# Up products of a two-stream feed-forward network by seven products in place of eight, on one Trainium2 core

## The chip, the cores and the metric

The kernel runs on one core of one Trainium2 chip. The metric is the device time of one execution in microseconds, as a median of several runs. In what follows TensorE is PE in the profile, VectorE is DVE, ScalarE is ACT, GpSimd is POOL, and SP issues the transfers. Weight loads of TensorE have a row of their own, PEld.

## The reference, cut to what matters

Two networks run one after the other on 512 tokens of width 1024, in fp32. The second works on two streams, X (512 tokens) and a context C (256 tokens). The part that is changed is the feed-forward network of its first layer, which both streams pass through with the same weights:

```python
def conv_ffn(h, w_up, conv, w_down):
    u = dwconv(h @ w_up, conv)          # 3 taps along the tokens, for each channel
    a, g = jnp.split(u, 2, axis=-1)     # 2 x 2816 channels
    return (jax.nn.silu(g) * a) @ w_down

x = x + g1 * y                          # y, yc: the convolution mixers
x = x + g2 * conv_ffn(modulate(rmsnorm(x, norm_ffn[l]), sh2, sc2), w_up[l], w_conv_ffn[l], w_down[l])
if not last:
    xc = xc + cg1 * yc
    xc = xc + cg2 * conv_ffn(modulate(rmsnorm(xc, norm_ffn[l]), csh2, csc2), w_up[l], w_conv_ffn[l], w_down[l])
```

Ahead of it are the mixers (their last product is `out`), behind it a windowed attention (`gqa`) in which C gives keys and values, and then the last feed-forward network, on X alone.

## The kernel before, in words

Every fp32 value that enters a matmul is held as two parts, high and low, and each product of two values is made by three matmuls (high by high, high by low, low by high: `mm3`). A split into parts is a cast (mostly on ScalarE) and a subtraction on VectorE (`split`). Activations lie with the channels on the 128 partitions, in 8 tiles of 128 channels, and the tokens in the columns.

The 2816 hidden channels are 22 units of 128. In `ffn` (line 1352) unit j needs two weight tiles of 1024 columns (`wload`: a transfer, a cast, a subtraction), and for gate and up 8 x 3 matmuls each, with 512 columns for X and 256 for C. The first two units (`HALVED`) run X in two halves of 256 columns. `act` makes the convolution out of PSUM (one scaled copy on ScalarE, two multiply-adds on VectorE), the silu, the product and the split. The units are taken in groups of 8, 7 and 7 (`GROUPS`); `down(g)` multiplies a group by its down weights, and each of its 8 x 2 results is added onto the residual (`resid`, VectorE). In the last group the last three output columns run C first, then X's first half, then its second half, so that the norm ahead of the attention (`modnorm`: statistics by `stat`, a reciprocal root `rstd`, its broadcast by TensorE `rstd_bc`, and the tiles `h_mod`) can start early.

The last feed-forward network, on X alone, already makes 17 of its 22 units by Strassen's method: X's tokens are two halves, the 1024 channels two halves, gate and up are the two halves of the weights, and seven products of sums take the place of eight (`wload7`, `products7`, lines 734 and 879). The 7 products are 7 x 4 x 3 matmuls. Sums of weights are made by VectorE for every unit, sums of activations once (`mod7`).

The order on the engines isn't the order of the code: all operations are recorded (class `Rec`) and listed by their dependences, with a modelled cost and a priority of their own for each. Weight splits have a bias of -1000000, `ahead(CHAIN)` puts chains to the norm first. All instructions bear the line of the one place that issues them (L385). `arenaR` holds split values, `arenaZ` and `arenaF` others, in addresses worked out for each stage (`phase`, `hold`, `t`); all transfers go through SP's queue.

Of the kernel before, what the change touches and what calls it, by code (L numbers as in the profile page):

```python
# [8 lines left out]
F32 = mybir.dt.float32  # L9
# [23 lines left out]
ROUNDS = 7  # L33
PLAIN = 5
WO1_AT = (2, 3, 5, 7)
SM_SCALE = 0.125
# [40 lines left out]
def _layout(i):  # L77
# [72 lines left out]
    o["wup1"] = fm(f("w_up_2")[1])  # L150
    o["wdn0"] = down(f("w_down_2")[0])
    o["wdn1"] = down(f("w_down_2")[1])
# [359 lines left out]
class Ker:  # L512
# [69 lines left out]
    def t(self, pool, shape, tag, dt=F32, bufs=1):  # L582

        n = 1
        for x in shape:
            n *= x
        c = self.hold(pool, n, tag, dt, bufs)
        m, off, n0, bufs, i = c
        assert n <= n0, (tag, n, n0)
        c[4] += 1  # L590
        o = off + (i % bufs) * (-(-n0 // GR) * GR)
# [141 lines left out]

    def wload7(self, src1, src2):
# [4 lines left out]
        a, b, c = (self.slot() for _ in range(3))  # L739
        d = [self.t("ph", [512], "whi22", F32R), self.t("z", [512], "wlo22", F32R)]  # L740
        s12, s34 = (self.t("ph", [1024], "wsum", bufs=2) for _ in range(2))
# [136 lines left out]

    def products7(self, st, w, one, two):


        nc = self.nc
        V = nc.vector
        x, y, z = (self.ps()[:, :TC] for _ in range(3))

        def product(p, n, first):
            (hi, lo), b = w[n - 1], st.b7[n - 1]
            for k in range(4):
# [3 lines left out]
        def keep(p):  # L892
            t = self.t("ph", [TC], "keep", bufs=4)
            nc.scalar.copy(t, p)
            return t

        def add(out, p, t):
            V.tensor_tensor(out=out, in0=p, in1=t, op=ALU.add)

# [6 lines left out]
        product(y, 3, False)  # L906
        add(one[:, TWO], y, s2)
        product(x, 7, False)
        add(two[:, TWO], x, s5)
        product(z, 2, True)  # L910
        add(one[:, ONE], z, s1)
        product(x, 4, False)
        nc.scalar.copy(two[:, ONE], x)

# [444 lines left out]
    def ffn(self, streams, wu, wd, conv=None, gate=None, post=None, mid=None, seven=None):  # L1359
# [5 lines left out]
        if True:  # L1365
# [3 lines left out]
            def up(j):  # L1369
                if seven is not None and j >= PLAIN:  # L1370
                    w = self.wload7(wu[j + NH - first], wu[j + first])
                    pu, pg = (self.t("ph", [S], "ft512", bufs=7) for _ in range(2))
                    self.products7(X, w, pu, pg)
                    acts[X, j] = self.act(None, X, pg, pu, j, conv, "z")
# [107 lines left out]
    def gqa(self, X, C, cfg):  # L1482
# [260 lines left out]
    def mixers(self, X, C):  # L1743
# [3 lines left out]
        if True:  # L1747
# [65 lines left out]
            def out(half):  # L1813
                order = [(mp, st) for mp in range(1 if half else 4) for st in streams]
# [3 lines left out]
                for mp, st in order:  # L1818
                    if mp not in ws:
# [4 lines left out]
                    for m2 in range(2):  # L1824
                        m = 2 * mp + m2
                        p = self.ps()[:, :st.T]
                        for k in range(4):
                            sl = slice(k * 256 + m2 * P, k * 256 + (m2 + 1) * P)
                            self.mm3(p, (hi[:, sl], lo[:, sl]), y[st, 4 * half + k], k == 0, k == 3)
                        self.resid(st, m, p, gate(st, m))  # L1830
                        if half:
                            self.stat(st, m)
                            if st is C and m == 2:
                                self.modnorm(X, 0, 1, ALL, ("mq512", 2))

# [38 lines left out]
    def run(self):  # L1874
# [59 lines left out]
        C.x = [xc[:, k, :] for k in range(KT)]  # L1934
        C.h = [(hc[0][:, k, :], hc[1][:, k, :]) for k in range(KT)]
        if start >= 5:
            load_x(lambda k: self.stat(X, k))
# [6 lines left out]
        if start <= 6:  # L1944
            self.phase({"g": list(range(8))}, (2 * KT * TC, KT * TC), 4)
            self.modnorm(C, 0, 1)
            self.segment("R")
            self.ffn([X, C], a["wup0"], a["wdn0"], conv="cf0",
                     gate=lambda st, m: self.modp[0][:, st.cond, 5, m:m + 1],
                     post=lambda st, m, tk: self.stat(st, m, tk), mid=lambda st, tk: self.modnorm(st, 1, 0, tk))  # L1950
        if stop == 6:
# [92 lines left out]
```

## Time and profile before

| what | value |
|---|---|
| median of three runs | 2578.2 us (2577.62 to 2578.24) |
| the profiled execution | 2579.19 us, of which 2577.4 us is the span |
| mean granted clock of TensorE | 0.997 |
| TensorE, matmuls | 2543.6 us, 99% |
| TensorE, weight loads | 2288.3 us, 89% |
| VectorE | 1964.1 us, 76% |
| ScalarE | 1304.7 us, 51% |

The two-stream feed-forward network lies between about 1370 and 1950 us of the span, the last one between about 2170 and 2570 us. In a group of matmuls the mean duration of one counts its pipelined end; the distance from one start to the next is shorter. A time behind an arrow is idle time of the engine ahead of an instruction, and what ended it.

### The profile page before, as it was taken

Reading aid. Unit: us, or ns where it says so; the run is one execution under the profiler, and the core shown is the slowest. Engines: PE = TensorE matmul, PEld = TensorE weight load, DVE = VectorE, ACT = ScalarE, POOL = GpSimd, SP = SyncE. Lnnn points to the kernel's source line nnn. Section 1 sums busy time; section 2 is a strip of 40 time slices with the busy share of each in tenths; the row PEclk is TensorE's granted clock in tenths of the full one; section 3 lists DMA queues with packets and bytes.
Section 4 is the critical chain, followed back from the end, with each engine's and each line's share of the span. In section 5 each row is a group of like instructions: output and inputs, shape, how many; then the busy total and the mean of one; then the engine's idle time right before and its main releaser. Section 6 shows DMA issues by size and latency. Waiting matters only on the chain.

```text
span 2577.4 us, 40702 instructions
## 1 busy us (share of the span) xinstructions
PE 2543.6 (99%) x15878; PEld 2288.3 (89%) x15878; DVE 1964.1 (76%) x3691; ACT 1304.7 (51%) x2481; POOL 130.7 (5%) x252
## 2 busy tenths in 40 slices
PE   8999999999999999999999999999999999999998
PEld 8998988889979888889888988888889988998997
DVE  8888999845898999448986754453457799997977
ACT  6877522224896322236664432231335798554644
POOL 0000000000010000004740000000000000000000
PEclk9999999999999999999999999999999999999999
DMA  4112566522124666321121121211112101223322
GB/s 148 56 62 72 190 211 221 181 94 78 58 66 153 206 222 197 117 93 60 58 74 55 57 66 66 66 62 65 63 56 66 50 26 50 92 78 95 123 89 84
DMA packets 73345, 252.92 MB, mean 98 GB/s; under 512 B 8512, under 2 KB 10688, under 8 KB 72768
## 3 DMA queue, kind: packets, MB, share of 16 engines
q1 hardware_dynamic: 73152, 250.32, 29.9%
q8 instruction: 124, 2.03, 0.3%
q14 instruction: 69, 0.57, 0.1%
HBM read 248.19 MB, written 2.10 MB: 97 GB/s over the span
## 4 chain that ended last, share of the span: by engine, by line
PE 92%; DVE 3%; POOL 2%; ACT 2%; issue 1%; DMA 0%; POOLq 0%; SPq 0%; DVEq 0%; ACTq 0%
PE psum_t L385 92%; POOL arenaZ L385 2%; DVE arenaF L385 2%; DVE arenaR L385 1%; ACT arenaF L385 1%; ACT arenaR L385 1%; DMA arenaF<-in_wup_dram 0%; ACT L383 0%; DMA arenaF<-in_xT_dram 0%; ACT L385 0%; DMA out_dram<-arenaF 0%; ACT arenaZ L385 0%; DVE psum_t L385 0%; DVE arenaZ L385 0%; POOLq L385 0%
## 5 line engine op out<-in xcount | busy, mean ns | idle before, releaser
L385 PE MATMUL psum_t<-arenaR 128*128 128x256 f32 (+2 forms) x13755 | 2352.0, 327 | 13.4 <-ACT arenaR L385 8.0
L385 PEld LDWEIGHTS psum_t<-arenaR 128*128 128x128 f32 x13755 | 2041.1, 189 | 240.0 <-ACT arenaR L385 9.7
L385 ACT CAST arenaR<-arenaF 128x1024 fp32r<-128x1024 f32 (+4 forms) x552 | 482.1, 881 | 740.2 <-PE psum_t L385 566.3
L385 DVE TENSOR_TENSOR arenaR<-arenaF,arenaR 128x1024 fp32r<-128x1024 f32 (+4 forms) x519 | 540.3, 1049 | 92.9 <-ACT arenaR L385 88.9
L385 ACT ACTIVATE arenaF<-arenaF 128x256 f32<-128x256 f32 (+10 forms) x809 | 428.7, 547 | 202.3 <-DVE arenaF L385 169.8
L385 DVE SCALAR_TENSOR_TENSOR arenaF<-psum_t,arenaF 128x511 f32<-128x511 f32 (+4 forms) x348 | 211.2, 611 | 247.1 <-PE psum_t L385 125.3
L385 DVE TENSOR_TENSOR arenaF<-arenaF 128x512 f32<-128x512 f32 (+5 forms) x503 | 266.5, 544 | 28.7 <-ACT arenaF L385 21.2
L385 DVE TENSOR_TENSOR arenaF<-psum_t,arenaF 128x512 f32<-128x512 f32 (+1 forms) x287 | 163.1, 576 | 137.8 <-PE psum_t L385 136.1
L385 PE MATMUL psum_t<-arenaZ,arenaR 128*128 128x256 f32 (+3 forms) x1261 | 261.7, 313 | 2.4 <-DVE arenaF L385 1.5
L385 DVE CUSTOM_DVE_ANT_0 arenaF<-arenaF 128x1024 f32<-128x1024 f32 x192 | 245.9, 1281 | 8.9 <-DMA arenaF<-in_wmod_dram 3.5
L385 PEld LDWEIGHTS psum_t<-arenaZ,arenaR 128*128 128x128 f32 x1261 | 189.2, 188 | 18.7 <-DVE arenaF L385 2.8
L385 ACT CAST arenaR<-psum_t 128x512 fp32r<-128x512 f32 (+3 forms) x333 | 157.6, 479 | 30.8 <-PE psum_t L385 27.6
L385 ACT ACTIVATE arenaF<-psum_t,arenaF 128x256 f32<-128x256 f32 (+3 forms) x170 | 85.9, 519 | 114.5 <-PE psum_t L385 105.4
L385 DVE SCALAR_TENSOR_TENSOR arenaF<-arenaF 128x256 f32<-128x256 f32 (+8 forms) x346 | 137.8, 421 | 4.7 <-ACT arenaF L385 3.0
L385 POOL TENSOR_TENSOR arenaZ<-arenaZ,arenaF 128x256 f32<-128x256 f32 x120 | 104.1, 869 | 446.9 <-DVE arenaF L385 423.6
L385 PE MATMUL psum_t<-arenaF 128*128 128x128 f32 (+2 forms) x730 | 113.7, 268 | 6.7 <-DVE arenaF L385 5.2
L385 DVE CUSTOM_DVE_ANT_0 arenaF<-psum_t,arenaF 128x256 f32<-128x256 f32 (+3 forms) x208 | 103.6, 511 | 11.7 <-PE psum_t L385 9.9
L385 DVE TENSOR_TENSOR arenaR<-psum_t,arenaR 128x512 fp32r<-128x512 f32 (+4 forms) x169 | 98.7, 590 | 12.1 <-ACT arenaR L385 10.6
L385 POOL COPY arenaF<-arenaF 128x1 f32<-128x1 f32 x128 | 26.4, 231 | 1595.1 <-DVE arenaF L385 1171.1
L385 PEld LDWEIGHTS psum_t<-arenaF 128*128 128x128 f32 x730 | 90.0, 152 | 17.4 <-DVE arenaF L385 6.2
L385 ACT ACTIVATE arenaR<-arenaF 128x256 fp32r<-128x256 f32 (+1 forms) x168 | 81.5, 523 | 31.9 <-DVE arenaF L385 24.9
L385 DVE SCALAR_TENSOR_TENSOR arenaR<-arenaF,arenaR 128x256 fp32r<-128x256 f32 (+1 forms) x164 | 77.7, 505 | 7.4 <-ACT arenaR L385 7.2
(49 smaller groups left out, 534.4 us busy)
## 6 DMA issues: line engine op xcount, KB each, us to landing
arenaF<-in_wmod_dram SPq DMA_DIRECT2D x96, 512.0 KB, 4.2
arenaF<-in_wgu_dram SPq DMA_DIRECT2D x88, 512.0 KB, 3.5
arenaF<-in_wup_dram SPq DMA_DIRECT2D x88, 512.0 KB, 3.4
arenaF<-in_wqkv_dram SPq DMA_DIRECT2D x35, 512.0 KB, 3.5
arenaF<-in_wd_dram SPq DMA_DIRECT2D x32, 448.0 KB, 3.2
arenaF<-in_wdn_dram SPq DMA_DIRECT2D x32, 448.0 KB, 3.2
arenaF<-in_wab_dram SPq DMA_DIRECT2D x20, 512.0 KB, 3.5
arenaF<-in_wd_dram SPq DMA_DIRECT2D x16, 512.0 KB, 4.2
```

The costliest lines, as they stand in the source:

```text
L385: getattr(getattr(self.nc, e), fn)(*a, **k)
```

## The change

X and C are joined to 768 columns, two halves of 384 (256 of X and 128 of C each). Three units are made plainly on the halves, nineteen by the seven products (`ffn_wide`). The weight sums are made in place (`wload7` with `place`). The tiles and sums of activations are made by `wide_first`, inside the mixers' last product, and `wide_rest`. Activations are kept for two units at a time, and the down product runs for each pair (the last four units together), with the down weights laid out for this. The last down product holds back six output columns in place of three. In the mixers' last product X runs in halves for six of eight output columns. The attention's fourth weight buffer gets another address.

```diff
+WIDE_PLAIN = 3
+WIDE_LAST = 6
@@ def wload7(self, src1, src2, place=False):
         a, b, c = (self.slot() for _ in range(3))
+        if place:
+            d = [self.t("ph", [512], f"w{x}22", F32R) for x in ("hi", "lo")]
...
+            self.dma(r1, src1)
+            self.dma(r2, src2)
+            (a11, a12), (a21, a22) = ((r[:, 0:512], r[:, 512:1024]) for r in (r1, r2))
+            self.split(r1, *a)
+            self.split(a22, *d)
+            V.tensor_tensor(out=a22, in0=a21, in1=a22, op=ALU.add)
+            V.tensor_tensor(out=a21, in0=a11, in1=a21, op=ALU.subtract)
+            V.tensor_tensor(out=a11, in0=a22, in1=a11, op=ALU.subtract)
+            V.tensor_tensor(out=a12, in0=a12, in1=a11, op=ALU.subtract)
+            self.split(r1, *b)
+            self.split(r2, *c)
...
+            return cut(a, 0), cut(a, 1), cut(b, 1), d, cut(c, 1), cut(b, 0), cut(c, 0)
@@ def products7(self, b7, w, one, two, segs=((0, TC, 0),), wide=TC):
-        x, y, z = (self.ps()[:, :TC] for _ in range(3))
+        x, y, z = (self.ps()[:, :wide] for _ in range(3))
...
+        def add(out, h, p, t):
+            for o, c in parts(out, h):
+                V.tensor_tensor(out=o, in0=p[:, c], in1=t[:, c], op=ALU.add)
...
+    SEGS = ((0, 256, 0), (256, 384, 512))
+    HALF = 384
+    def wide_half(self, h, js, tmp, dst):
+        for j in js:
+            t = tmp(j)
+            self.wide_scaled(h, j, t)
+            self.split(t, *dst(j))
...
+    def wide_first(self):
...
+        with self.ahead(CHAIN):
+            self.rstd(self.pair[0], ONE)
+            self.rstd_bc(self.pair[0], ONE)
+        self.wide_half(0, range(KT), ...
+    def wide_rest(self):
...
+        with self.ahead(CHAIN):
+            self.rstd(X, TWO)
+            self.rstd_bc(X, TWO)
...
+        self.wide_half(1, range(KT), ...
+        for k in range(4):
...
+            self.wide_scaled(0, k, t)
+            self.wide_scaled(0, k + 4, u)
+            V.tensor_tensor(out=t, in0=b12, in1=t, op=ALU.subtract)
+            self.split(t, *(x[:, k] for x in t1))
...
+    def ffn_wide(self, wu, wd, taps, gate, post, mid):
...
+        def up(j):
+            u, g = (self.t("ph", [768], "ft768") for _ in range(2))
+            if j >= WIDE_PLAIN:
+                w = self.wload7(wu[j], wu[j + NH], True)
+                self.products7(self.b7, w, u, g, self.SEGS, W)
+                return u, g
...
+        def act(j, u, g):
...
+            for x in seg:
+                self.conv3(t1[:, x], g[:, x], x.stop - x.start, taps, NH + j)
+            nc.scalar.activation(t1, t1, AF.Silu)
+            for x in seg:
+                self.conv3(t2[:, x], u[:, x], x.stop - x.start, taps, j)
+            V.tensor_tensor(out=t2, in0=t1, in1=t2, op=ALU.mult)
+            acts[j] = [self.t("z", [768], "aw", F32R, bufs=4) for _ in range(2)]
+            self.split(t2, *acts[j])
+        def down(js, last=False):
...
+            passes = [(C, ALL), (X, ONE), (X, TWO)]
+            n = WIDE_LAST if last else 0
+            order = [(m, y) for m in range(KT - n) for y in ((X, ALL), (C, ALL))]
+            order += [(m, y) for y in passes for m in range(KT - n, KT)]
+            for m, (st, tk) in order:
...
+                with self.ahead(CHAIN if last else 0):
+                    self.resid(st, m, p, gate(st, m), tk)
...
+                    if m == KT - n and (st, tk) in passes[1:]:
+                        mid(*passes[passes.index((st, tk)) - 1])
+        for j in range(NH):
...
+            ug = up(j)
+            if j > 1 and j % 2 == 0 and j < NH - 2:
+                down((j - 2, j - 1))
...
+        down(range(NH - 4, NH), True)
@@ gqa
-                at = lambda x: self.cls["ph", x][1] + NH % 9 * S
-                spare = {("ph", w): ["R", at(x), 1024, 1, 0] for w, x in (("whi3", "ah512"), ("wlo3", "al512"))}
+                at = self.cls["ph", "t2l"][1] - 512
+                spare = {("ph", w): ["R", at + x, 1024, 1, 0] for w, x in (("whi3", 0), ("wlo3", 1024))}
@@ mixers, out(half)
-                    order += [(mp, st) for st in streams for mp in range(1, 4)]
+                    order += [(mp, st, tk) for st, tk in ((C, ALL), (X, ONE), (X, TWO)) for mp in range(1, 4)]
...
+                            if tk is TWO and m == 2:
+                                self.wide_first()
@@ body
-            self.modnorm(C, 0, 1)
             self.segment("R")
-            self.ffn([X, C], a["wup0"], a["wdn0"], conv="cf0",
...
+            self.wide_rest()
+            self.ffn_wide(a["wup0"], a["wdn0"], "cf0", ...
```

Where this moves instructions is seen at two places. The first is TensorE's order inside the network. Before, 24 or 48 matmuls of X (512 columns) alternate with as many of C (256); the unit's weights are in `arenaR`, and the activations of C are in `arenaZ`:

```order
L385 MATMUL psum_t<-arenaR 128x512 x24
L385 MATMUL psum_t<-arenaZ_11793,arenaR 128x256 x24
L385 MATMUL psum_t<-arenaR 128x512 x24
L385 MATMUL psum_t<-arenaZ_11793,arenaR 128x256 x24
L385 MATMUL psum_t<-arenaR 128x512 x48
L385 MATMUL psum_t<-arenaR 128x256 x48
```

Now, on the same engine at the seam between the first two Strassen units; the product that reads the fourth block of weights is the one that takes a tile from `arenaZ` at 384 columns, and those of 512 and 256 columns are the down product of the pair before:

```order
L388 MATMUL psum_t<-arenaZ_11793,arenaR 128x384
L388 MATMUL psum_t<-arenaR 128x384 x30
L388 MATMUL psum_t<-arenaZ_11793,arenaR 128x512 x3
L388 MATMUL psum_t<-arenaZ_11793,arenaR 128x256 x3
L388 MATMUL psum_t<-arenaZ_11793,arenaR 128x512 x3
L388 MATMUL psum_t<-arenaZ_11793,arenaR 128x256 x3
L388 MATMUL psum_t<-arenaR 128x384 x2
L388 MATMUL psum_t<-arenaZ_11793,arenaR 128x512 x3
L388 MATMUL psum_t<-arenaR 128x384 x46
```

The two long alternations have become runs of 384 columns, and pieces of a down product stand between two products of one unit. Twenty-four of the thirty are the first two products of the next unit.

The second place is VectorE's order at the end of the network, from X's last residual addition (the first row of 256 columns that reads `psum_t`) on; a row with `arenaR` of 1024 columns is a weight split for the attention, one with `arenaR` of 256 columns a finished tile for it. Before:

```order
L385 SCALAR_TENSOR_TENSOR arenaF<-psum_t,arenaF 128x256
L385 SCALAR_TENSOR_TENSOR arenaR<-arenaF,arenaR 128x256 x2
L385 TENSOR_TENSOR arenaF<-arenaF 128x256
L385 SCALAR_TENSOR_TENSOR arenaF<-arenaF 128x256
L385 TENSOR_TENSOR arenaR<-arenaF,arenaR 128x1024
```

Now, on VectorE at the same place:

```order
L388 SCALAR_TENSOR_TENSOR arenaF<-psum_t,arenaF 128x256
L388 TENSOR_SCALAR arenaF<-psum_t 128x2
L388 TENSOR_TENSOR arenaR<-arenaF,arenaR 128x1024
L388 TENSOR_TENSOR arenaF<-arenaF 128x2
L388 TENSOR_TENSOR arenaF<-arenaF 128x256
L388 SCALAR_TENSOR_TENSOR arenaF<-arenaF 128x2
L388 TENSOR_TENSOR arenaR<-arenaF,arenaR 128x1024
L388 TENSOR_TENSOR arenaF<-arenaF 128x256
L388 SCALAR_TENSOR_TENSOR arenaF<-arenaF 128x2
L388 SCALAR_TENSOR_TENSOR arenaR<-arenaF,arenaR 128x256
L388 SCALAR_TENSOR_TENSOR arenaF<-arenaF 128x256
L388 TENSOR_TENSOR arenaF<-arenaF 128x256
```

Before, C's last two tiles stand right behind the last residual addition. Now the fourth of C's eight tiles is the tenth row, behind two weight splits, three statistics and the reciprocal root of X's first half; C's eighth tile comes ten rows further on.

## Rows read from the trace of the kernel before

**Rows 1.** The page: span, and busy time of engines, share, instructions.

```profile
span 2577.4 us, 40702 instructions
...
PE 2543.6 (99%) x15878; PEld 2288.3 (89%) x15878; DVE 1964.1 (76%) x3691; ACT 1304.7 (51%) x2481; POOL 130.7 (5%) x252
```

**Rows 2.** Windows: from:to, length, busy (instructions) of each engine, clock, DMA share, GB/s.

```profile
320.00:600.00 280.00, 280.00 (x1237) 231.86 (x1236) 218.48 (x315) 74.58 (x88) 3.73 (x12) 1.00 0.53 170
1380.00:1980.00 600.00, 597.87 (x3636) 536.61 (x3635) 323.84 (x524) 203.66 (x338) 0.00 (x0) 1.00 0.20 64
2168.00:2208.00 40.00, 34.94 (x237) 32.10 (x237) 32.62 (x75) 26.22 (x56) 0.55 (x4) 0.91 0.11 34
2248.00:2288.00 40.00, 40.00 (x337) 40.00 (x336) 37.02 (x58) 23.31 (x37) 0.00 (x0) 1.00 0.18 61
2408.00:2448.00 40.00, 40.00 (x251) 36.01 (x250) 38.15 (x57) 23.70 (x37) 0.00 (x0) 1.00 0.41 129
```

**Rows 3.** Groups of TensorE, 320 to 600 us: names, shapes, count | busy us, mean ns | idle.

```profile
L385 PE MATMUL psum_t<-arenaR 128*128 128x512 f32 x1237 | 280.5, 389 | 0.0
```

**Rows 4.** The same view of TensorE, 1440 to 1940 us.

```profile
L385 PE MATMUL psum_t<-arenaR 128*128 128x512 f32 x1421 | 330.1, 390 | 0.0
L385 PE MATMUL psum_t<-arenaR 128*128 128x256 f32 x1040 | 128.1, 283 | 0.0
L385 PE MATMUL psum_t<-arenaZ,arenaR 128*128 128x256 f32 x444 | 55.6, 280 | 0.0
```

**Rows 5.** The same view of TensorE, the whole span.

```profile
L385 PE MATMUL psum_t<-arenaR 128*128 128x512 f32 x5465 | 1309.1, 391 | 0.4 <-DVE arenaR L385 0.4
L385 PE MATMUL psum_t<-arenaR 128*128 128x256 f32 x7798 | 1030.2, 285 | 10.6 <-ACT arenaR L385 6.8 <-DVE arenaF L385 1.8 <-DVE arenaR L385 1.7
...
L385 PE MATMUL psum_t<-arenaR 128*128 128x384 f32 x32 | 8.5, 343 | 0.0
```

**Rows 6.** Timeline of TensorE at 2247 us: start, us, engine, operation, count.

```profile
2247.39 6.39 PE L385 MATMUL psum_t<-arenaR 128*128 128x256 f32 x52
```

**Rows 7.** Groups of VectorE, 1440 to 1940 us.

```profile
L385 DVE SCALAR_TENSOR_TENSOR arenaF<-psum_t,arenaF 128x511 f32<-128x511 f32 x84 | 63.0, 750 | 119.6 <-ACT arenaF L385 118.2
L385 DVE TENSOR_TENSOR arenaR<-arenaF,arenaR 128x1024 fp32r<-128x1024 f32 x47 | 57.6, 1225 | 23.7 <-ACT arenaR L385 23.5
L385 DVE SCALAR_TENSOR_TENSOR arenaF<-psum_t,arenaF 128x255 f32<-128x255 f32 x88 | 41.8, 478 | 0.9
...
L385 DVE SCALAR_TENSOR_TENSOR arenaF<-psum_t,arenaF 128x512 f32<-128x512 f32 x20 | 15.0, 751 | 53.5 <-PE psum_t L385 53.5
L385 DVE TENSOR_TENSOR arenaR<-arenaF,arenaR 128x512 fp32r<-128x512 f32 x22 | 15.0, 681 | 0.0
...
L385 DVE SCALAR_TENSOR_TENSOR arenaF<-psum_t,arenaF 128x256 f32<-128x256 f32 x20 | 9.7, 484 | 33.0 <-PE psum_t L385 33.0
```

**Rows 8.** Groups of VectorE, the whole span.

```profile
L385 DVE TENSOR_TENSOR arenaF<-psum_t,arenaF 128x256 f32<-128x256 f32 x119 | 48.4, 419 | 7.4 <-PE psum_t L385 6.2 <-ACT arenaF L385 0.4
...
L385 DVE TENSOR_TENSOR arenaR<-arenaF,arenaR 128x768 fp32r<-128x768 f32 x8 | 7.6, 955 | 2.3 <-ACT arenaR L385 2.3
...
L385 DVE TENSOR_TENSOR arenaR<-psum_t,arenaR 128x128 fp32r<-128x128 f32 x8 | 2.3, 286 | 0.1
```

**Rows 9.** Groups of ScalarE, 1440 to 1940 us.

```profile
L385 ACT CAST arenaR<-arenaF 128x1024 fp32r<-128x1024 f32 x46 | 48.2, 1048 | 129.8 <-PE psum_t L385 129.8
...
L385 ACT CAST arenaR<-arenaF 128x512 fp32r<-128x512 f32 x22 | 13.4, 610 | 0.0
```

**Rows 10.** Timeline of TensorE at both ends of the network; idle time in brackets.

```profile
1407.98 0.65 PE L385 MATMUL psum_t<-arenaF 128*128 128x128 f32 x4 [0.84 <-DVE arenaF L385]
...
1957.15 0.43 PE L385 MATMUL psum_t<-arenaF 128*128 128x128 f32 x2 [0.65 <-DVE arenaF L385]
```

**Rows 11.** Timeline of VectorE at 1409 us and 1956 us.

```profile
1409.29 1.41 DVE L385 SCALAR_TENSOR_TENSOR arenaF<-arenaF 128x512 f32<-128x512 f32 x2
...
1956.30 0.16 DVE L385 TENSOR_SCALAR arenaF<-psum_t 128x2 f32<-128x2 f32 x1 [1.15 <-ACT arenaF L385]
```

More of the change, by code (lines that the diff above doesn't have):

```diff
@@ L590, in t @@
         c[4] += 1
-        o = off + (i % bufs) * (-(-n0 // GR) * GR)
+        o = off[i % bufs] if isinstance(off, list) else off + (i % bufs) * (-(-n0 // GR) * GR)
         self.rec.fresh.update((m, x, y) for x in range(o // GR, (o + n - 1) // GR + 1) for y in (0, 1))
@@ L892, in keep, with parts @@
         def keep(p):
-            t = self.t("ph", [TC], "keep", bufs=4)
+            t = self.t("ph", [wide], "keep", bufs=4)
             nc.scalar.copy(t, p)
             return t
-        def add(out, p, t):
-            V.tensor_tensor(out=out, in0=p, in1=t, op=ALU.add)
+        def parts(out, h):
+            for c0, c1, o in segs:
+                o += h * (c1 - c0)
+                yield out[:, o:o + c1 - c0], slice(c0, c1)
+        def add(out, h, p, t):
+            for o, c in parts(out, h):
+                V.tensor_tensor(out=o, in0=p[:, c], in1=t[:, c], op=ALU.add)
         product(x, 1, True)
@@ L906, in products7 @@
         product(y, 3, False)
-        add(one[:, TWO], y, s2)
+        add(one, 1, y, s2)
         product(x, 7, False)
-        add(two[:, TWO], x, s5)
+        add(two, 1, x, s5)
         product(z, 2, True)
-        add(one[:, ONE], z, s1)
+        add(one, 0, z, s1)
         product(x, 4, False)
-        nc.scalar.copy(two[:, ONE], x)
+        for o, c in parts(two, 0):
+            nc.scalar.copy(o, x[:, c])
+    SEGS = ((0, 256, 0), (256, 384, 512))
[5 more added lines that the diff above has]
+            self.split(t, *dst(j))
@@ new lines, in wide_scaled @@
+    def wide_scaled(self, h, j, t):
+        nc = self.nc
+        for st, (c0, c1, _) in zip(self.pair, self.SEGS):
+            n = c1 - c0
+            tk = slice(h * n, h * n + n)
+            nc.vector.scalar_tensor_tensor(out=t[:, c0:c1], in0=st.x[j][:, tk], scalar=self.moda[0][:, st.cond, 1, j:j + 1],
+                                           in1=st.rbc[:, tk], op0=ALU.mult, op1=ALU.mult)
+            nc.scalar.activation(t[:, c0:c1], t[:, c0:c1], AF.Identity, bias=self.modp[0][:, st.cond, 3, j:j + 1])
@@ new lines, in wide_first @@
+    def wide_first(self):
+        off = self.cls["hp", "h"][1]
+        n = 4 * self.HALF
+        tile_ = lambda x: self.ar["R"][:, off + x * n:off + (x + 1) * n].rearrange("p (k t) -> p k t", t=self.HALF)
+        self.w11, self.w21 = (tile_(0), tile_(1)), (tile_(2), tile_(3))
+        self.w22 = [tile_(4)]
+        with self.ahead(CHAIN):
+            self.rstd(self.pair[0], ONE)
+            self.rstd_bc(self.pair[0], ONE)
+        self.wide_half(0, range(KT), lambda j: self.t("ph", [S], "mq512", bufs=2)[:, :self.HALF],
+                       lambda j: [x[:, j % 4] for x in (self.w21 if j >= 4 else self.w11)])
@@ L1813, in out @@
             def out(half):
-                order = [(mp, st) for mp in range(1 if half else 4) for st in streams]
+                order = [(mp, st, ALL) for mp in range(1 if half else 4) for st in streams]
                 if half:
-                    order += [(mp, st) for st in streams for mp in range(1, 4)]
+                    order += [(mp, st, tk) for st, tk in ((C, ALL), (X, ONE), (X, TWO)) for mp in range(1, 4)]
                 ws = {}
-                for mp, st in order:
+                for mp, st, tk in order:
                     if mp not in ws:
@@ L1825, in out @@
                         m = 2 * mp + m2
[L1826 removed]
+                        p = self.ps()[:, :st.T if tk is ALL else TC]
                         for k in range(4):
                             sl = slice(k * 256 + m2 * P, k * 256 + (m2 + 1) * P)
[L1829 to L1830 removed]
+                            self.mm3(p, (hi[:, sl], lo[:, sl]), [x[:, tk] for x in y[st, 4 * half + k]], k == 0, k == 3)
+                        self.resid(st, m, p, gate(st, m), tk)
                         if half:
[L1832 to L1834 removed]
+                            for t in (ONE, TWO) if st is X and tk is ALL else (tk,):
+                                self.stat(st, m, t)
+                            if tk is ONE and m == 2:
+                                with self.ahead(CHAIN):
+                                    self.rstd(C)
+                                    self.rstd_bc(C)
+                            if tk is TWO and m == 2:
+                                self.wide_first()
             self.rec.bias -= 300
@@ L1935, in run @@
         C.h = [(hc[0][:, k, :], hc[1][:, k, :]) for k in range(KT)]
+        self.pair = X, C
         if start >= 5:
```

104 lines of the change are left out of this document (96 added, 8 removed).

## The prediction, made before the result was known

> **What bounds the kernel now.** I read the page's busy table first: TensorE is busy 2543.6 us of a span of 2577.4 us, VectorE 1964.1 us [rows 1]. So nearly all time is matmul time, and a saving counts where TensorE is the engine that never waits. That is asked stage by stage with the table of windows [rows 2]: in the 600 us that hold the two-stream feed-forward network TensorE is busy 597.87 us and VectorE 323.84 us, and what TensorE waits for there, about 2 us, lies at the two ends. In the middle the list of matmuls shows 1421 of 512 columns and 1484 of 256 and no idle time ahead of them [rows 4]. A matmul less is therefore time less, until another engine becomes late.
>
> The price of a matmul is its start-to-start distance, not its own mean, which counts the pipelined end too. In 320 to 600 us TensorE runs 1237 matmuls of 512 columns without a gap [rows 2, 3]: 280.00/1237 = 226.4 ns. Of 256 columns, 52 in a row take 6.39 us [rows 6]; less one own length of 0.285 us [rows 5] that is 6.105/51 = 119.7 ns. The two prices give 1421 x 226.4 + 1484 x 119.7 = 499.3 us for a window of 500 us, so they hold in this stage.
>
> A matmul of 384 columns runs nowhere before in a long row. Half way between the two prices it costs 173.1 ns. By columns alone it would be 0.75 x 226.4 = 169.8. Its own mean, 343 ns, lies 5 ns above the middle of 285 and 391 [rows 5], which would make it 178. I take 174, nearest the interpolation, and keep 169.8 and 178 as ends.
>
> **The change part by part.** *Matmuls.* Before, one hidden unit (gate and up) takes 48 matmuls of 512 and 48 of 256 columns; the first two units run X in halves, so over 22 units there are 960 of 512 and 1248 of 256. After, three plain units take 96 of 384 each and nineteen units 7 x 4 x 3 = 84 of 384 each: 288 + 1596 = 1884. Two smaller edits split X into halves: six output columns in the mixers' last product turn 72 matmuls of 512 into 144 of 256, and the last down product (six output columns of four units, 24, in place of three of seven, 21, with three matmuls each) turns 9 more into 18. The net is -1041 of 512, -1086 of 256, +1884 of 384:
> 1041 x 226.4 = 235.7, 1086 x 119.7 = 130.0, 1884 x 174 = 327.8, so 365.7 - 327.8 = **37.9 us less** (45.8 at 169.8, 30.3 at 178). All of it lies in a stage where TensorE doesn't wait, so it counts in full if nothing new is late.
>
> The Trainium skill's page "TensorE: Matmul & The Clock Gate", section "Back-to-back issue gap", names for streams of weight load and matmul 81 ns at 128 columns and 131 ns at 512, that is, a large price for each instruction and a small one for each column; on the straight line through its two figures, an estimate, the change would save only about 27 us, and the time would be some 2557 us. The trace does not agree: 226.4 ns at 512 and 119.7 at 256 is nearly all columns, and the rule gets 0.01, inside the dear end of rival (c).
>
> *VectorE in the steady stretch.* It gets new work: per Strassen unit three splits of weights 1024 wide (1.225 us each), five operations 512 wide (one split, four sums: 0.68), three additions of two products in parts of 256 and 128 (0.419 + 0.286), eight convolution steps (four of 0.750, four of 0.478), and one product and one split 768 wide (0.955) [rows 7, 8]: 3.68 + 3.40 + 2.12 + 4.91 + 1.91 = 16.0 us. Per pair of units: 32.0, and two splits of down weights 2.45, and eight residual additions for each stream (0.751 + 0.484), 9.88: together 44.4 us by durations in 66 instructions. Neighbours overlap: two that last 0.75 each take 1.41 us together [rows 11], 0.08 less for each instruction, so VectorE is held 39.1 us per pair. TensorE has for the pair 168 x 0.174 = 29.2 and for the down product 48 x (0.2264 + 0.1197) = 16.6, together 45.8 us. That is 85%. In the last network, which already works by Strassen's method, VectorE is busy 37.02 and 38.15 us in windows of 40, and TensorE 40.00 in both [rows 2]: 93 and 95% have been carried without a wait. So I price the steady stretch at 0.5 us (ends: 0, and 19 us as worked out under the rivals). ScalarE has less to do than VectorE in every one of these rows and is hidden behind it. The transfers use 0.20 of the DMA engines' time in the stage [rows 2], and SP's queue has two issues fewer; they stay hidden.
>
> *A wait that the in-place weights add.* The fourth block of weights has one buffer, and its split waits for the seventh product of the unit before; four sums and two splits 1024 wide are queued behind it in the same tiles. The chain from there to the block that product 5 of the next unit needs (the second product in the code): cast 0.610, split 0.68, two sums 1.36, cast 1.048, split 1.225 [rows 7, 9], together 4.9 us. TensorE's order puts 30 matmuls of 384 columns, the first of which ends the seventh product, and 12 of the down product between (the first places of the order above): 29 x 0.174 = 5.0, 6 x (0.2264 + 0.1197) = 2.1, together 7.1 us. Between the two units of a pair the rest of the down product lies there. So nothing is lost, with 2.2 us to spare; without this cover, in the code's order, the chain would cost 4.9 less one product (12 x 0.174 = 2.1), 2.8 us a unit.
>
> *The start.* TensorE now begins with 384-wide halves, and VectorE makes the tiles of the first half ahead of it, the second half and the sums while three plain units (50 us) and the first down product run. Before, TensorE waits 0.84 us for the reciprocal root there [rows 10], and all its idle time in the stage is 2.1 us. Now there are two reciprocal roots (of C and of X's first half) ahead of the first unit. I take 1.5 us more than before; ends -1 and +5, since the tiles, the first weights and the sums all fall to VectorE there, and no row prices them together.
>
> *The end.* The last down product holds back six output columns instead of three, in the passes C, X first half, X second half. A pass is shorter than VectorE's part of it: behind X's last residual addition there now stand, up to C's eighth tile for the attention, three weight splits of 1.225, twelve operations of 0.484, five of 0.419 and five of two columns, 0.16 each [rows 7, 8, 11] (the second place shown of the order, and ten rows beyond it): 3.7 + 5.8 + 2.1 + 0.8 = 12.4 us by durations, less 25 x 0.08, 10.4 us. TensorE has 48 matmuls of 256 columns, 5.75 us, of its own in this time. The difference, 4.6 us, is waited for in several short waits; before it is 0.65 us [rows 10]. So +4 us; ends +1 and +8.
>
> *The rest.* The fourth weight buffer at another address and the layout of the down weights move no work; the attention behind them keeps its instructions and changes their order a little: 0, ends -1.5 and +1.5.
>
> Sum: -37.9 + 0.5 + 1.5 + 4 = -31.9 us on the profiled execution's 2579.2 us, which is 1.0 above the median 2578.2; against the median 2578.2 - 31.9 = 2546.3. I forecast **2546 us**.
>
> **The rivals.** (a) *VectorE becomes the bound of the stage.* For it speaks the 85% and that convolution, residual and weight splits all go through it in a fixed order, so a late residual makes a late weight. If it can't do better than the 93% of the last network and the overlap is lost, a pair takes 44.4/0.93 = 47.7 us in place of 45.8, and 9.5 pairs lose 18 us: 2546 + 18 = 2564. Against it: the two windows of the last network in [rows 2], in which VectorE was fuller and TensorE waited for nothing.
>
> (b) *Slower than before: the fourth block's chain.* If TensorE's cover above fails, because VectorE comes to the chain late by its other work, each of the nineteen units waits 2.8 us for the chain: 2546 + 53 = 2599. From 32/19 = 1.7 us a unit the gain is gone. For it: one buffer, and waits in a row may also bring the clock down, as in 2168 to 2208 us, where TensorE waits 5 us and the granted clock is 0.91 [rows 2]. Against it: those 2.2 us to spare.
>
> (c) *The matmul is dearer than thought or half the saving is taken back:* 178 ns and both ends at their worst: -30.3 + 0.5 + 5 + 8 = -17, 2561. Or cheaper: 169.8 with free ends: 2578.2 - 45.8 + 1 = 2533.
>
> (d) *The change does nothing*: the saving would have to be hidden. TensorE's 40.00 of 40 speaks against it.
>
> **How the numbers follow.** The forecast's own case, 2537 to 2554, has 0.68. Rival (a) and the dear end of (c), 2554 to 2568, together 0.19; the cheap end of (c), 2530 to 2537, 0.06; no change 0.03; (b) 0.04. The range from 2536 to 2560 leaves out about 2 in 10. What is under 0.2% (5 us) can't be told from no change in this kernel: faster 0.93, same 0.03, slower 0.04.
>
> **What would show it.** In the profile after: windows of 40 us in the wide network with TensorE at 40.00 and VectorE at 33 to 35; the mean of a 384-column matmul about 345 ns with no idle time ahead; the stage shorter by 32 to 36 us; waits of 4 to 5 us in sum where the attention begins, for VectorE; 1 to 4 us at the stage's start. Waits for weights at each unit would make it wrong by (b), waits for residuals or sums spread over the pairs by (a), and a spacing of 384 columns off 174 ns by (c).

## The result, and the profile after

The changed kernel takes 2540.9 us (median of four runs, 2539.6 to 2543.1) and the kernel before, beside it, 2578.2 us. The ratio is 0.9855 with an interval of 0.9838 to 0.9872: 37 us faster, where 32 had been forecast.

The busy table of the page after shows where: TensorE gives up 38.4 us, VectorE takes on 173 us, and the span follows TensorE [rows 1].

```profile
span 2537.9 us, 40742 instructions
...
PE 2505.2 (99%) x15635; PEld 2288.5 (90%) x15635; DVE 2137.0 (84%) x4081; ACT 1383.5 (55%) x2664; POOL 133.4 (5%) x252
```

Windows of the changed network (from:to, length, busy time of TensorE, weight loads, VectorE, ScalarE and GpSimd, granted clock, DMA share, GB/s): its start, its steady stretch and its end.

```profile
1400.00:1440.00 40.00, 39.91 (x263) 39.22 (x262) 38.57 (x104) 34.88 (x93) 0.00 (x0) 1.00 0.09 27
1440.00:1480.00 40.00, 40.00 (x232) 37.97 (x231) 38.34 (x66) 26.84 (x55) 0.00 (x0) 1.00 0.17 54
1560.00:1760.00 200.00, 200.00 (x1155) 190.60 (x1154) 174.74 (x297) 85.44 (x136) 0.00 (x0) 1.00 0.21 69
1890.00:1950.00 60.00, 56.19 (x427) 54.15 (x426) 50.75 (x121) 35.22 (x77) 0.00 (x0) 0.97 0.20 65
```

TensorE never waits in the 200 us of the third row, with VectorE at 87%, against 54% over the network before [rows 2]. At the start (first two rows) VectorE is fuller, 96%, and TensorE waits 0.09 us in 80; at the end (last row) it does wait.

The matmuls of the steady stretch, by shape (count | busy us, mean ns | idle ahead):

```profile
L388 PE MATMUL psum_t<-arenaR 128*128 128x384 f32 x670 | 124.5, 335 | 0.0
L388 PE MATMUL psum_t<-arenaZ,arenaR 128*128 128x512 f32 x224 | 60.2, 392 | 0.0
L388 PE MATMUL psum_t<-arenaZ,arenaR 128*128 128x256 f32 x228 | 34.3, 279 | 0.0
L388 PE MATMUL psum_t<-arenaZ,arenaR 128*128 128x384 f32 x33 | 11.0, 335 | 0.0
```

With the old prices for 512 and 256 columns, 224 x 226.4 + 228 x 119.7 = 78.0 us, 122.0 us are left for 703 matmuls of 384: 173.5 ns each. A row of the timeline agrees, 39 of them in 6.92 us, (6.92 - 0.335)/38 = 173.3:

```profile
1576.69 6.92 PE L388 MATMUL psum_t<-arenaR 128*128 128x384 f32 x39
```

The account goes by three fixed points on VectorE: the last residual addition of the two-stream network, that of the last network, and the last VectorE operation. In the kernel before:

```profile
1968.34 0.48 DVE L385 SCALAR_TENSOR_TENSOR arenaF<-psum_t,arenaF 128x256 f32<-128x256 f32 x1
...
2566.81 0.48 DVE L385 SCALAR_TENSOR_TENSOR arenaF<-psum_t,arenaF 128x256 f32<-128x256 f32 x1
...
2573.50 0.75 DVE L385 TENSOR_SCALAR arenaF<-psum_t,arenaF 128x512 f32<-128x512 f32 x1 [1.20 <-DMA out_dram<-arenaF]
```

The same three points of the changed kernel (the last row holds two operations that last 1.41 us together; the second is the third point):

```profile
1926.96 0.49 DVE L388 SCALAR_TENSOR_TENSOR arenaF<-psum_t,arenaF 128x256 f32<-128x256 f32 x1 [0.17 <-PE psum_t L388]
...
2528.85 0.48 DVE L388 SCALAR_TENSOR_TENSOR arenaF<-psum_t,arenaF 128x256 f32<-128x256 f32 x1
...
2532.12 1.41 DVE L388 TENSOR_SCALAR arenaF<-psum_t,arenaF 128x512 f32<-128x512 f32 x2
```

| stretch | before | after | difference | forecast |
|---|---|---|---|---|
| to the network's last residual | 1968.3 | 1927.0 | -41.4 | -35.9 |
| from there to the last network's last residual | 598.5 | 601.9 | +3.4 | +4 |
| from there to the last VectorE operation | 6.7 | 3.9 | -2.8 | 0 |
| from there to the span's end | 3.9 | 5.1 | +1.2 | 0 |

The sum, -39.6, is that of the two profiled executions. The one before is 1.0 us above its median and the changed one 1.2 us below, so the sum is larger than the 37.3 us between the medians.

TensorE's waits where the attention begins (in brackets, with what ended them) are, but for the last one, for VectorE, as foreseen: 3.7 us in sum, 2.9 of them behind the last residual, where the kernel before had 0.65 us [rows 10]. The granted clock of these 60 us is 0.97; 3% of 60 us is some 1.8 us more, an estimate.

```profile
1919.04 0.43 PE L388 MATMUL psum_t<-arenaF 128*128 128x128 f32 x2 [0.83 <-DVE arenaF L388]
...
1927.60 1.67 PE L388 MATMUL psum_t<-arenaR 128*128 128x256 f32 x12 [0.67 <-DVE arenaF L388]
1930.32 1.10 PE L388 MATMUL psum_t<-arenaR 128*128 128x256 f32 x7 [1.05 <-DVE arenaR L388]
...
1933.37 0.58 PE L388 MATMUL psum_t<-arenaR 128*128 128x256 f32 x2 [0.81 <-DVE arenaR L388]
1934.29 1.36 PE L388 MATMUL psum_t<-arenaR 128*128 128x256 f32 x6 [0.34 <-ACT arenaR L388]
```

### The profile page after: what moved, and what is told of

The parts are those of the page before. It is cut to its first block, busy times and chain, and to the rows that moved or that the text cites. A ratio compares the mean times of both kernels' runs of the same rounds, so it can differ in the third digit from the quotient of the medians.

```text
span 2537.9 us, 40742 instructions
## 1 busy us (share of the span) xinstructions
PE 2505.2 (99%) x15635; PEld 2288.5 (90%) x15635; DVE 2137.0 (84%) x4081; ACT 1383.5 (55%) x2664; POOL 133.4 (5%) x252
## 4 chain that ended last, share of the span: by engine, by line
PE 93%; DVE 3%; POOL 2%; ACT 1%; issue 1%; DMA 0%; DVEq 0%; POOLq 0%; SPq 0%; ACTq 0%
PE psum_t L388 93%; POOL arenaZ L388 2%; DVE arenaF L388 2%; DVE arenaR L388 1%; ACT arenaR L388 1%; ACT arenaF L388 1%; DMA arenaF<-in_xT_dram 0%; ACT L388 0%; DVE psum_t L388 0%; ACT L386 0%; ACT arenaZ L388 0%; DVEq L2243 0%; DVE arenaZ L388 0%; POOLq L388 0%; SPq L388 0%
## 5 line engine op out<-in xcount | busy, mean ns | idle before, releaser
L388 PE MATMUL psum_t<-arenaR 128*128 128x256 f32 (+3 forms) x12968 | 2214.9, 324 | 15.1 <-ACT arenaR L388 8.2
L388 PEld LDWEIGHTS psum_t<-arenaR 128*128 128x128 f32 (+1 forms) x12968 | 1946.1, 188 | 186.6 <-ACT arenaR L388 10.5
L388 ACT CAST arenaR<-arenaF 128x512 fp32r<-128x512 f32 (+5 forms) x599 | 516.4, 871 | 752.1 <-PE psum_t L388 520.8
L388 DVE TENSOR_TENSOR arenaR<-arenaF,arenaR 128x1024 fp32r<-128x1024 f32 (+5 forms) x563 | 577.0, 1034 | 80.0 <-ACT arenaR L388 77.0
L388 PE MATMUL psum_t<-arenaZ,arenaR 128*128 128x256 f32 (+2 forms) x1805 | 397.6, 333 | 2.4 <-DVE arenaF L388 1.5
L388 DVE TENSOR_TENSOR arenaF<-arenaF 128x512 f32<-128x512 f32 (+7 forms) x585 | 325.2, 568 | 21.6 <-ACT arenaF L388 15.7
L388 DVE TENSOR_TENSOR arenaF<-psum_t,arenaF 128x256 f32<-128x256 f32 (+2 forms) x401 | 199.6, 512 | 169.2 <-PE psum_t L388 167.9
L388 PEld LDWEIGHTS psum_t<-arenaZ,arenaR 128*128 128x128 f32 x1805 | 291.1, 188 | 35.3 <-DVE arenaF L388 3.1
L388 DVE SCALAR_TENSOR_TENSOR arenaF<-arenaF 128x511 f32<-128x511 f32 (+9 forms) x556 | 245.0, 474 | 4.9 <-ACT arenaF L388 3.4
L388 DVE SCALAR_TENSOR_TENSOR arenaF<-psum_t,arenaF 128x256 f32<-128x256 f32 (+3 forms) x293 | 167.1, 595 | 32.1 <-PE psum_t L388 30.7
```

Source lines behind the costliest of these rows:

```text
L388: getattr(getattr(self.nc, e), fn)(*a, **k)
```

## The experiments

Four questions were open: is the gain the columns alone, how much room VectorE has, why the start lost its waits, and where the two ends' microseconds come from. Times are medians; each ratio is to runs of the kernel before on the same chip, which took 2579 us.

**Is it the columns?** All units plain:

```diff
-WIDE_PLAIN = 3
+WIDE_PLAIN = 22
```

> All 22 units made plainly on the two halves of 384 columns, everything else as changed (pairs, joined streams, the sums of activations are still made but not used). Theory (the gain is the columns saved by the seven products): 19 units take 12 matmuls of 384 more each, 228 x 0.173 = 39.4 us, so about 2580 us, within 3 us of the kernel before. Rival (part of the gain is from the pairs, the joined halves or the start): the time stays clearly below before, by 5 us or more.

Measured: 2576.7 us, ratio 0.9991 (0.9982 to 1.0001). The theory holds: without the seven products nothing is left that the timing can tell from no change. Pairs, joined streams and halves of 384 columns are in the main the form in which they fit.

The trace says more. The start is as free as in the changed kernel, and the last stretch is 3.9 us there too, so these two small gains, of which more below, don't come from the seven products. The attention's beginning, in contrast, has only 0.95 us of waits, the longest 0.35 us, though the last down product holds back the same six columns:

```profile
1400.00:1440.00 40.00, 39.91 (x266) 39.20 (x265) 38.45 (x105) 34.57 (x94) 0.00 (x0) 1.00 0.09 27
1974.19 3.25 PE L388 MATMUL psum_t<-arenaR 128*128 128x256 f32 x25 [0.35 <-DVE arenaR L388]
2565.52 0.47 DVE L388 SCALAR_TENSOR_TENSOR arenaF<-psum_t,arenaF 128x256 f32<-128x256 f32 x1
2568.78 1.41 DVE L388 TENSOR_SCALAR arenaF<-psum_t,arenaF 128x512 f32<-128x512 f32 x2
```

From this kernel to the changed one the medians fall by 35.8 us. The sum of what differs comes near it: 228 matmuls of 384 columns at 173.5 ns, 39.6 us, less what the end costs more in the changed kernel, 2.8 us of waits and some 1.8 us of clock, is 35.0.

**How much room has VectorE?** The low part of the activations is written again on VectorE, twice in every unit (e4), twice in units 6 to 15 alone (e5), four times in those (e6). The diff is e4's:

```diff
             self.split(t2, *acts[j])
+            for _ in range(2):
+                V.tensor_tensor(out=acts[j][1], in0=t2, in1=acts[j][0].bitcast(F32), op=ALU.subtract)
```

> The changed kernel with two more subtractions 768 wide for each unit on VectorE (the same value written again): 2 x 0.87 us a unit, VectorE's share in the steady stretch from 85 to 93 per cent. Theory (VectorE has room): no more than 2 us slower, 2541 to 2543 us, TensorE still at 40.00 of 40. Rival (VectorE already sets the pace in places): half or more of the added 3.5 us a pair shows, 17 us or more, 2558 us.

Measured: 2558.5 us, ratio 0.9917 (0.9903 to 0.9930). The rival's number, to the microsecond, and the theory's was wrong. But the place isn't the rival's. Some 8 of the 17.7 us lie at the start, a wait of 4.27 us and the clock; 3.2 us are three new waits ahead of the end, from 1914 to 1921 us. In the steady stretch there is one wait of 1.31 us and then a short one for each of five pairs.

```profile
1440.00:1480.00 40.00, 35.73 (x190) 34.05 (x189) 35.13 (x60) 25.66 (x54) 0.00 (x0) 0.91 0.14 41
1560.00:1760.00 200.00, 198.35 (x1137) 188.27 (x1136) 184.85 (x305) 84.66 (x134) 0.00 (x0) 1.00 0.23 70
1600.00:1640.00 40.00, 39.59 (x228) 37.23 (x227) 37.22 (x61) 15.99 (x23) 0.00 (x0) 1.00 0.22 66
```

Its timeline of TensorE names the waits in the first and the last window: the first down product's activations come 4.27 us late, and the clock falls with it; at 1604 us it is 0.41 us. The extra operations stand in the chain to the activations themselves, so the 4.27 us hold that delay as well as VectorE's fullness.

```profile
1470.26 6.13 PE L388 MATMUL psum_t<-arenaZ,arenaR 128*128 128x512 f32 x17 [4.27 <-DVE arenaZ L388]
...
1604.42 1.86 PE L388 MATMUL psum_t<-arenaR 128*128 128x384 f32 x9 [0.41 <-DVE arenaR L388]
```

So the load was put into the steady units alone:

> The changed kernel with the two extra subtractions 768 wide in units 6 to 15 alone, 17.4 us more VectorE work in the steady stretch. Theory (the loss of the last such run lay at the two ends, where VectorE was already at 38.5 of 40; in the steady stretch 93 per cent costs one wait of 0.6 us a pair): 2 to 4 us slower than the changed kernel, about 2544 us. Rival (VectorE sets the pace everywhere): half of the 17.4 us, 9 us slower, 2550 us.

Measured: 2542.4 us, ratio 0.9858 (0.9843 to 0.9873). That is 1.5 us over the changed kernel, which the scatter of the runs doesn't tell from nothing, with TensorE at 200.00 of 200. The rival falls; of the theory the place holds, and even the small waits that it priced didn't come.

> The same with four extra subtractions in units 6 to 15, 35 us more, VectorE's share in the steady stretch 100 per cent. Theory (VectorE has about 7 us of room a pair, and then it is the bound): the first half is nearly free, of the second half some shows: 5 to 14 us slower, 2546 to 2555 us. Rival (it sets the pace everywhere): 17 us or more, 2558 us.

Measured: 2550.8 us, ratio 0.9892 (0.9879 to 0.9906), 10 us slower. The same 200 us in both runs (e5 first):

```profile
1560.00:1760.00 200.00, 200.00 (x1151) 190.22 (x1150) 186.24 (x303) 86.23 (x135) 0.00 (x0) 1.00 0.22 69
```

```profile
1560.00:1760.00 200.00, 195.47 (x1110) 182.66 (x1109) 190.46 (x308) 85.89 (x134) 0.00 (x0) 1.00 0.21 64
```

VectorE at 93% costs TensorE nothing over these five pairs; asked for more, it gets to 95% and TensorE loses 4.5 us in 200. The limit isn't sharp: in e4, with the extra load from the first unit on, TensorE lost 0.41 us a pair, 1%, with VectorE at 92%. So the changed kernel, at 87%, has some 5% of room in the steady stretch, and at the start, by e4 and by e10 below, hardly any. Why the same load costs a little in e4 and nothing in e5 was not isolated.

**Why is the start free of waits?** First the mixers' halves alone, on the kernel before:

```diff
-                    order += [(mp, st) for st in streams for mp in range(1, 4)]
+                    order += [(mp, st, tk) for st, tk in ((C, ALL), (X, ONE), (X, TWO)) for mp in range(1, 4)]
...
-                            if st is C and m == 2:
-                                self.modnorm(X, 0, 1, ALL, ("mq512", 2))
+                            if tk is TWO and m == 2:
+                                self.modnorm(X, 0, 1, ONE, ("mq512", 2))
...
+            self.modnorm(X, 0, 1, TWO)
             self.modnorm(C, 0, 1)
```

> The kernel before, with only this part of the change: in the mixers' last product X runs in halves for six of eight output columns, in the order C, X first half, X second half, and X's norm is made half by half. Theory (the waits at the network's start went away because the first half's norm can start early): 0.8 us more matmuls, about 3 us less waits, so 2 to 3 us faster than before, 2575 to 2576 us. Rival (they went away because the network begins with other tiles): no change or slower, 2578 to 2580 us.

Measured: 2578.6 us, ratio 0.9999 (0.9990 to 1.0008). The theory falls: the halves by themselves bring nothing. TensorE is still idle for 1.1 us in 40, where the kernel before has 1.5, and the longest two waits are these:

```profile
1407.85 0.43 PE L385 MATMUL psum_t<-arenaF 128*128 128x128 f32 x2 [0.46 <-DVE arenaF L385]
...
1416.54 2.19 PE L385 MATMUL psum_t<-arenaR 128*128 128x256 f32 x15 [0.43 <-ACT arenaR L385]
```

Then the time of C's root, in the changed kernel (e9), and the halves undone in it (e12):

```diff
# e9
-                            if tk is ONE and m == 2:
+                            if tk is TWO and m == 2:
                                 with self.ahead(CHAIN):
                                     self.rstd(C)
# e12
-                    order += [... for st, tk in ((C, ALL), (X, ONE), (X, TWO)) for mp in range(1, 4)]
+                    order += [... for st, tk in ((C, ALL), (X, ALL)) for mp in range(1, 4)]
...
-                            if tk is ONE and m == 2:
+                            if st is X and m == 2:
                                 with self.ahead(CHAIN):
...
-                            if tk is TWO and m == 2:
+                            if st is X and m == 7:
                                 self.wide_first()
```

> The changed kernel with the reciprocal root of C asked for where X's second half begins, not a pass earlier. Theory (the network's start lost its waits because both roots are asked for while the mixers' last product still runs behind them): VectorE gets C's parts of the first eight tiles later, TensorE waits 1 to 2 us there, 2542 to 2543 us. Rival (the wide tiles alone made the start free): no change, 2540 to 2542 us, and no wait over 0.3 us in the trace.

Measured: 2542.3 us, ratio 0.9856 (0.9842 to 0.9871). This time would fit the theory as well as no change; the trace decides. It has one wait, of 0.17 us, where 1 to 2 us had been foreseen: the theory falls again.

> The changed kernel with X whole again in the mixers' last product (C, then X with 512 columns), so that X's first half and its root come only behind all of X. 0.8 us less matmuls. Theory (the halves give TensorE 8.6 us of other work behind the first half's root, which together with the wide tiles frees the start): without them TensorE waits for the last statistics, the root and the first tiles, 4 to 7 us, so 2544 to 2547 us. Rival (the wide tiles alone free it, as the late root of C suggests): no wait of more than 1 us more, 2540 to 2541 us.

Measured: 2547.3 us, ratio 0.9881 (0.9865 to 0.9898), 6 us slower. Here the theory holds: in the timeline of TensorE X's statistics and root stand alone behind the mixers' last product, 5.8 us of waits in four pieces, and the clock of the stretch falls to 0.91.

```profile
1414.57 0.61 PE L388 MATMUL psum_t<-arenaF 128*128 128x1 f32 x4 [2.29 <-DVE arenaF L388]
1416.03 0.77 PE L388 MATMUL psum_t<-arenaF 128*128 128x1 f32 x4 [0.85 <-DVE arenaF L388]
1417.02 0.69 PE L388 MATMUL psum_t<-arenaF 128*128 128x128 f32 x2 [0.22 <-DVE arenaF L388]
...
1420.15 0.66 PE L388 MATMUL psum_t<-arenaF 128*128 128x128 f32 x2 [2.44 <-DVE arenaF L388]
```

```profile
1400.00:1440.00 40.00, 34.20 (x174) 31.30 (x173) 34.73 (x95) 30.92 (x85) 0.00 (x0) 0.91 0.05 14
```

The start needs both, the halves and the wide tiles; halves without wide tiles (e3) leave waits of about 1 us, wide tiles without halves (e12) make them longer. Why wide tiles do with the halves what X's and C's own tiles don't was not isolated.

**What costs at the end?** The number of output columns held back:

```diff
-WIDE_LAST = 6
+WIDE_LAST = 3    # e2; 8 in e8
```

> The last down product holds back three output columns, not six. Theory (the short passes put VectorE behind at the end, 5.8 us of waits where the attention begins): passes of half the length are covered worse or better; if VectorE's list behind the last residual is what counts, its length stays and the time moves by no more than 3 us either way, with the waits still 3 us or more. Rival (holding back six is what costs it): the waits fall to the 0.8 us of the kernel before and the time falls by 4 to 5 us, to 2536.

Measured: 2543.7 us, ratio 0.9861 (0.9848 to 0.9875); in the traces 2.3 us more than the changed kernel to the network's last residual, counted from the last residual of the first feed-forward network. The rival falls: shorter passes are no remedy. The waits are four long ones, 5.4 us.

> The changed kernel with all eight output columns of the last down product held back, not six. 0.3 us more matmuls. Theory (a longer pass gives VectorE more time before the attention needs the tiles: three columns 2.3 us dearer than six in the trace): the waits at the end fall by 1 to 2 us, 2539 to 2541 us. Rival (VectorE's list behind the last residual is what counts, and it doesn't get shorter): no change or 0.3 us slower.

Measured: 2537.2 us, ratio 0.9838 (0.9825 to 0.9852), its runs from 2536.1 to 2537.6 all below the changed kernel's. Theory: yes, and by more than it said. Two waits are left, 1.25 us, and the clock of the 60 us stays at 1.00:

```profile
1901.59 3.16 PE L388 MATMUL psum_t<-arenaR 128*128 128x256 f32 x24 [0.98 <-ACT arenaR L388]
...
1932.07 1.81 PE L388 MATMUL psum_t<-arenaR 128*128 128x256 f32 x13 [0.27 <-DVE arenaR L388]
```

```profile
1890.00:1950.00 60.00, 58.68 (x477) 57.86 (x476) 53.15 (x128) 37.65 (x81) 0.00 (x0) 1.00 0.22 68
```

With three, six and eight columns held back the waits are 5.4, 3.7 and 1.25 us. Two tasks run at once here, one pass's matmuls and the tiles of the pass before; the longer the pass, the more of VectorE's list fits beside it. This kernel is faster than both, the one before and the changed one.

**The last stretch.** On the kernel before, only the rotation of weight buffers:

```diff
         if start <= 7:
+            self.wslot += 1
             self.gqa(X, C, 2)
```

> The kernel before, with only the weight buffers' rotation one further on from the second attention on. No work is added or removed. Theory (2.75 us of the gain lie behind the last residual and come from the rotation, since the last network's columns 4 and 5 no longer share a buffer): 2 to 3 us faster than before, the time from the last residual addition to the last VectorE operation 3.9 us in place of 6.7. Rival (that piece varies by itself): no change, 2578 to 2580 us.

Measured: 2576.9 us, ratio 0.9994 (0.9985 to 1.0003). By its times alone no change is not excluded; by the trace the stretch is that of the changed kernel, 3.9 us from the last residual to the last VectorE operation:

```profile
2564.54 0.48 DVE L385 SCALAR_TENSOR_TENSOR arenaF<-psum_t,arenaF 128x256 f32<-128x256 f32 x1
...
2567.80 1.41 DVE L385 TENSOR_SCALAR arenaF<-psum_t,arenaF 128x512 f32<-128x512 f32 x2
```

The new network leaves the rotation elsewhere, so that columns 4 and 5 of the very last down product, a network later, no longer share a weight buffer; column 5's weights come earlier, and X's first half is done before the last matmul. That this sharing is the whole reason was read from the order, not tried alone.

**Can more be had?** From e8 on:

```diff
 # e10: WIDE_LAST = 8 and
-WIDE_PLAIN = 3
+WIDE_PLAIN = 2
 # e11: WIDE_LAST = 8 and self.wslot += 1 ahead of the attention, as in e7
```

> All eight output columns held back, and two plain units in place of three: 12 matmuls of 384 less, 2.1 us. Theory (from 1400 to 1480 us VectorE is at 38.5 of 40 and has no room; a Strassen unit in place of a plain one adds 4.7 us of weight work there and the sums are wanted 16.6 us earlier): waits of 3 to 8 us appear, so 1 to 6 us slower than with eight columns and three plain units, 2538 to 2543 us. Rival (VectorE can put the plain units' convolutions off): 2 us faster, 2535 us.

Measured: 2546.4 us, ratio 0.9870 (0.9853 to 0.9886), 9 us slower than e8. The theory's sign, and more than its size: the two longest waits are 2.71 and 2.29 us, and the clock falls again. ScalarE ends both. Ahead of the first it had itself waited 1.98 us for VectorE; ahead of the second VectorE waits 1.11 us for ScalarE, so there VectorE's list isn't the whole cause (the second pair of rows below).

```profile
1454.72 3.94 PE L388 MATMUL psum_t<-arenaR 128*128 128x384 f32 x13 [2.71 <-ACT arenaF L388]
...
1468.26 2.21 PE L388 MATMUL psum_t<-arenaZ,arenaR 128*128 128x512 f32 x7 [2.29 <-ACT arenaZ L388]
```

```profile
1450.91 1.46 ACT L388 CAST arenaR<-arenaF 128x1024 fp32r<-128x1024 f32 x2 [1.98 <-DVE arenaF L388]
...
1465.67 0.96 DVE L388 TENSOR_TENSOR arenaF<-arenaF 128x768 f32<-128x768 f32 x1 [1.11 <-ACT arenaF L388]
```

Its window, with the clock:

```profile
1440.00:1480.00 40.00, 34.76 (x177) 31.66 (x176) 36.05 (x67) 26.90 (x54) 0.00 (x0) 0.91 0.18 54
```

> All eight output columns held back, and the weight buffers' rotation one further on from the second attention on. The order behind the last residual stays the good one. Theory (the rotation is worth 1 to 3 us in the attention and nothing else moves): 2534 to 2540 us, the stretch from X's last residual of the network to the attention's last changes by up to 2 us either way. Rival (the rotation mattered only at the end): within 0.5 us of the kernel with eight columns, 2537 us.

Measured: 2537.7 us, ratio 0.9839 (0.9825 to 0.9854). As e8: the rotation brings this kernel nothing. Both the rival and the theory's range hold this time, so the run doesn't tell them apart.

## Why the prediction was right

*The matmuls* were the gain, as the sum had it. 384 columns cost 173.5 ns, not 174, so the term is -38.8 in place of -37.9 (a matmul's own mean is 335 ns, where 345 had been named as a sign). e1 shows that the rest of the change, without them, is worth 2.6 us by the medians, and nothing for certain.

*The steady stretch* was priced at 0.5 us and cost none. The share of VectorE, forecast at 85%, is 87%; that 93 to 95% would still be free was read from the last network's windows, and e4, e5 and e6 put the limit near there, between 92 and 95%. So rival (a) failed by some 5% of VectorE's time only. (Its price is 18 us by its own working; the 19 us in the paragraph on the steady stretch is a slip.) Rival (b), the wait for the fourth block, didn't come: no idle time stands ahead of any 384-column matmul in the steady stretch.

*The start* is the step that failed in sign. It was priced at +1.5 us, since nothing in the trace priced the tiles together; the idle 1.5 us of before (the 2.1 us that the prediction names hold 0.65 us of the end) became 0.1. The step asked how many roots stand ahead of the network and not what TensorE still has to do beside each: with X in halves there are 72 matmuls of 256 columns, 8.6 us, behind the first half's last product. e12 takes these away and finds 5.8 us of waits. The worry about the other engines' lists was sound all the same: e4 and e10 add a little to them and lose some 8 to 9 us there, waits and clock together.

*The end* was right in place and sign, 3.4 us where 4 had been said, but the number is near in part by luck. The waits behind the last residual are 2.9 us and not 4.6; the lower clock, some 1.8 us, had not been priced; and some 1.3 us of the sum come back elsewhere in the 600 us of that stretch, where was not found. The cause is half right: e8 shows that the length of the passes counts, but e1 has the same passes and 0.95 us of waits. Behind its last residual one weight split for the attention stands among the tiles on VectorE, where the changed kernel has three (e1's first):

```profile
1974.13 1.22 DVE L388 TENSOR_TENSOR arenaR<-arenaF,arenaR 128x1024 fp32r<-128x1024 f32 x1
```

```profile
1927.43 1.22 DVE L388 TENSOR_TENSOR arenaR<-arenaF,arenaR 128x1024 fp32r<-128x1024 f32 x1
...
1929.04 1.22 DVE L388 TENSOR_TENSOR arenaR<-arenaF,arenaR 128x1024 fp32r<-128x1024 f32 x1
...
1933.63 1.22 DVE L388 TENSOR_TENSOR arenaR<-arenaF,arenaR 128x1024 fp32r<-128x1024 f32 x1
```

So it is probably short passes together with a VectorE that comes to them late; the second part was not tried alone.

*The last stretch*, 2.8 us, was counted as untouched, as it holds the same instructions; its buffers aren't the same (e7), and 1.2 us of it go back in the transfer at the end.

All of these errors lie on the same side: 0.9 us for the matmuls, 0.5 for the steady stretch, 2.9 for the start, 0.6 for the end and 1.6 for the last stretch are 6.5 of the 7.7 us between -31.9 and the -39.6 of the profiled executions. The other 1.2 us, ahead of the network's last residual, were not located. The medians are 5.4 us from the forecast.

## What to carry to other kernels

Where one engine never waits, count its work at measured prices: here that gave the result within a few per cent. Then spend the effort on the seams, where the new stage starts and ends, since there the other engines were fullest and the longer waits cost the clock as well. Ask of a chain of norm and root what the busy engine still has to do beside it, and make that piece longer, as eight columns held back did here. And a rotation of buffers carries a change of one stage into stages that it doesn't touch.

## What was not expected of the hardware

Short waits took the granted clock down with them. Around waits of 4.27 us (e4), of 2.71, 0.25 and 2.29 us (e10), and of 2.29, 0.85, 0.22 and 2.44 us (e12) the 40 us have a granted clock of 0.91, that is, the 1.2 GHz level for a part of them; 9% of 40 us is 3.6 us, beside 4.3 to 5.8 us of waits. The changed kernel's five waits at the attention, none over 1.05 us, still have 0.97 in 60 us. A wait of 0.98 us with little near it (e8) left the clock at 1.00, and so did the 4.5 us that e6 lost in 200 us by waits of 0.8 us and less.
